# A Strassen MLP's first block: sums interleaved with x differences, w2's first casts moved to GpSimd, last stores moved to SyncE's queue

## The chip, the cores and the metric

The kernel runs on one core of one Trainium2 chip. The metric is the device time of one execution in microseconds (us), and smaller is better. "Median of n runs" is over the executions that were timed.

## The reference

```python
def reference(x, w1, w2):            # x [8, 1024, 1024], w1 [1024, 4096], w2 [4096, 1024], float32
    h = x @ w1
    h = 0.5 * h * (1 + np.tanh(np.sqrt(2 / np.pi) * (h + 0.044715 * h ** 3)))
    return (h @ w2).astype(np.float32)
```

## The kernel before

x is worked on in 8 superblocks of 1024 rows. Both matrix products use Strassen's scheme: 7 products of half-size blocks in place of 8, paid for with sums of weight blocks and differences of x blocks. Operands are 16-bit. (The second product of the first superblock is the exception, done with 8 plain products, as w2's sums are not made yet.)

The *first superblock* is unlike the others, and this case is about it. Besides its own products it loads w1 and w2 as float32, casts them, keeps w1's casts in DRAM (`raw_d`), makes w2's sums and stores them (`w_d`), casts the next superblock's x to 16 bits in DRAM (`x_cast`) and loads that transposed (`x_transpose`). The second superblock loads `raw_d` again and makes and stores w1's sums. From the third on, all sums come ready from DRAM.

Loads and most stores are issued by SyncE, in program order (`load_in_order`). GpSimd issues `x_cast`, the stores of w1's sums and the output's stores. Parts that the change touches (cuts marked `# ...`):

```python
up  = tile_pool(name="up", bufs=26)   # 16-bit units of 128x2048: x blocks, weights, sums ("u")
gcp = tile_pool(name="gcp", bufs=4)   # float32 staging tiles ("gc")
tp  = tile_pool(name="tp", bufs=10)   # 128x512 float32 results ("tmp")
# ...
def cast_in(dst, src, cast):          # float32 load into one of the 4 staging tiles, then a cast
    st = gcp.tile([P] + list(dst.shape[1:]), F32, name="gc")
    load_in_order(st, src)
    cast(out=dst, in_=st)
# ...
def load_cols(self, c, n):            # first quarter of w1, by columns
    cs = slice(c * P, (c + n) * P)
    for b, t in self.raw.items():
        # ... cast_in, blocks of the left half on ScalarE, of the right half on GpSimd
    for m in SUMS:
        self.sum(m, cs)
# ...
def x_first():
    # ... for each 128 rows:
            xn = gcp.tile([P, 2, HT], F32, name="gc")
            load_in_order(flat(xn), x2[r0:r0 + P, :])
            # ... transposed on TensorE, cast out of PSUM by ScalarE and DVE
# ...
def matmul2_first(sb, g, keep_w1, xb):
    for b in range(2):                                   # column halves of the output
        for q in range(NI // QC):                        # quarters of w2's rows
            # ... cast_in(raw..., w2v[...], nc.scalar.copy): w2 on ScalarE
            # ... products of this quarter into 8 banks
            if b == 0:
                # ... keep; if q == 0: keep_w1()
            else:
                # ... w2's sums on DVE
                if q in (1, 2):
                    write(q - 1)                         # 7 stores of 512 KB: w_d
        if b == 1:
            blocks = x_transpose(xb, load_in_order)      # 16 transposing loads
            write(2); write(3)
        for i in range(2 * NQ):
            # ... last 3 products of each bank, then
            o = temp()
            # ... copied out by ScalarE (i odd) or DVE (i even), and stored
# ...
blocks = x_first()
for sb in range(NSB):
    xs = x_sums(blocks)                                  # 5 differences on DVE
    g, quad = matmul1(xs, sb)
    if sb == 0:
        xb = x_cast(1, pool_last[0])                     # behind GpSimd's last cast so far
        last, blocks = matmul2_first(sb, g, quad.keep_raw, xb)
        continue
    # ...
```

Of the kernel before, what the change touches and what calls it, by code (L numbers as in the profile page):

```python
# [8 lines left out]
F32 = mybir.dt.float32  # L9
# [4 lines left out]
SUB = mybir.AluOpType.subtract  # L14
P = 128
# [38 lines left out]
def kernel(  # L54
# [48 lines left out]
    def unit(rows, cols):  # L103
        return up.tile([P, rows, cols], DT, name="u")

    def tt(out, in0, in1, op):
        nc.vector.tensor_tensor(out=out, in0=in0, in1=in1, op=op)  # L107
# [6 lines left out]
    def load_in_order(out, in_, **kw):  # L114
        return tc.keep_in_program_order(nc.sync.dma_start(out=out, in_=in_, **kw))  # L115
# [18 lines left out]
    def cast_in(dst, src, cast):  # L134
# [3 lines that stand above are left out]
# [4 lines left out]
    class MadeQuad:  # L142
# [22 lines left out]
        def load_cols(self, c, n):  # L165

            cs = slice(c * P, (c + n) * P)
            for b, t in self.raw.items():
                k0 = (int(b[0]) - 1) * KH
                for k in range(0, KH, KH // n):  # L170
                    cast_in(
                        t[:, k:k + KH // n, cs],
                        w1v[int(b[1]) - 1, :, k0 + k:k0 + k + KH // n, cs],
                        nc.scalar.copy if b[1] == "1" else pool_copy,
                    )
            for m in SUMS:
                self.sum(m, cs)

        def sum(self, m, sl=slice(None)):
            make_sum(self.ops, m, self.raw, KH, QW, sl)  # L180
# [18 lines left out]



    def x_sums(blocks):
        ops = {3: blocks["11"], 4: blocks["22"]}
        for m in (5, 1, 2, 7, 6):
            u, v = A_TERMS[m]
            ops[m] = unit(KH, HT)
            tt(ops[m], blocks[u], blocks[v], SUB)
        return ops

    def x_blocks():  # L210
        return {b: unit(KH, HT) for b in ("22", "21", "12", "11")}

    def x_first():
        identity = consts.tile([P, P], F32, name="identity")
        make_identity(nc, identity)
        blocks = x_blocks()
        for a in (1, 0):
            for q in range(NQ):
                r0 = a * HT + q * P
                xn = gcp.tile([P, 2, HT], F32, name="gc")  # L220
                load_in_order(flat(xn), x2[r0:r0 + P, :])
                for k in (1, 0):
                    ps = psum()
                    for j in range(KH):
                        nc.tensor.matmul(  # L225
                            ps[:, j * P:(j + 1) * P],
                            lhsT=xn[:, k, j * P:(j + 1) * P],
                            rhs=identity,
                            is_transpose=True,
                            start=(j == 0),  # L230
                            stop=(j == KH - 1),
                        )
                    eng = nc.vector.tensor_copy if k == 0 else nc.scalar.copy
                    eng(
                        out=blocks[f"{a + 1}{k + 1}"][:, :, q * P:(q + 1) * P],
                        in_=ps.rearrange("p (j t) -> p j t", t=P),
                    )
        return blocks

    def x_cast(s, after):  # L240
        xb = xdram.tile([SB, H], DT, name="xb")
# [19 lines left out]
    def matmul1(xs, sb):  # L261
        g = {b: gp.tile([P, NI, HT], GT, name=f"g{b}") for b in ("11", "12", "21", "22")}

        def product(bank, w, m, first, last):
            ops, cs = w
            for k in range(KH):
                nc.tensor.matmul(  # L267
                    bank,
                    lhsT=ops[m][:, k, cs],
                    rhs=xs[m][:, k, :],  # L270
                    start=(first and k == 0),
                    stop=(k == KH - 1),
                    skip_group_check=not first,
                )

        def gelu(b, c, src):
            nc.scalar.activation(out=g[b][:, c, :], in_=src, func=GELU)

        late = None

        def finish(c, w, q, s2):
            product(q, w, 6, False, True)
            c22 = temp()
            tt(c22, q, s2, ADD)
            gelu("22", c, c22)

        quads = []

        def ahead(q, step):

            if q == NI // QC:
                return
            if sb > 1:
                if step == 0:
                    quads.append(load_ops(w1_d[q], (4, 5, 1, 2, 3, 7, 6), KH, QW))
                return
            if step == 0:
                quad = MadeQuad(q, sb == 0)
                quads.append(quad)
                if sb == 0:  # L300
                    quad.load()
                    quads[q - 1].keep_raw()
            for m in ((), (4,), (1, 3), (7, 6))[step]:
                quads[q].sum(m)
            if sb == 1 and step == 3:
                quads[q].copy_plain()

        if sb == 0:
            quads.append(MadeQuad(0, True))
            for c, n in ((0, 1), (1, 1), (2, 2)):  # L310
                quads[0].load_cols(c, n)
        else:
            for step in range(QC):
                ahead(0, step)

        for c in range(NI):
            q, j = divmod(c, QC)
            if j == 0:
                ahead(q + 1, 0)
            w = (quads[q] if sb > 1 else quads[q].ops, slice(j * P, (j + 1) * P))  # L320
            pb, qb = psum(), psum()
            product(pb, w, 4, True, False)
            v = temp()
            nc.scalar.copy(out=v, in_=pb)  # L324
            product(qb, w, 5, True, False)
            u = temp()
            tt(u, v, qb, SUB)
            if late is not None:
                finish(*late)
            rb = psum()  # L330
            product(rb, w, 1, True, False)
            s = temp()
            tt(s, u, rb, ADD)
            product(pb, w, 2, False, True)
            gelu("21", c, pb)
            s2 = temp()
            tt(s2, s, pb, SUB)
            product(qb, w, 3, False, False)
            gelu("12", c, qb)
            product(rb, w, 7, False, True)  # L340
            c11 = temp()
            tt(c11, u, rb, ADD)
            gelu("11", c, c11)
            late = (c, w, qb, s2)
            if j:
                ahead(q + 1, j)
        finish(*late)
        return g, quads[-1]
# [3 lines left out]
    def store(sb, b, q, src):  # L352
        r0 = sb * SB + (int(b[0]) - 1) * HT + q * P
        o0 = (int(b[1]) - 1) * OH
        return nc.gpsimd.dma_start(out=out2[r0:r0 + P, o0:o0 + OH], in_=src)  # L355

    def matmul2_first(sb, g, keep_w1, xb):


        TAIL = 3  # L360
# [8 lines left out]
        for b in range(2):  # L369
# [13 lines left out]
            for q in range(NI // QC):  # L383
                raw = raw_units(QC, OH, (b + 1,))
                for j in range(0, QC, 2):
                    c = q * QC + j
                    for a in range(2):
                        cast_in(
                            raw[f"{a + 1}{b + 1}"][:, j:j + 2, :],
                            w2v[b, a, :, c:c + 2, :],  # L390
                            nc.scalar.copy,
                        )
                for j in range(QC):
                    w = [raw[f"{a + 1}{b + 1}"][:, j, :] for a in range(2)]
                    ready.append(w)
                    if q * QC + j < NI - TAIL:
                        for i in range(2 * NQ):
                            mm(i, q * QC + j, w)
                if b == 0:
                    keep.append(raw)  # L400
                    if q == 0:
                        keep_w1()
                else:
                    ops = {}
                    for m in SUMS + PLAIN:
                        make_sum(ops, m, {**keep[q], **raw}, QC, OH)
                    made.append(ops)
                    if q in (1, 2):
                        write(q - 1)
# [66 lines left out]
            last = store(sb, "11", q, c11)  # L476
        return last

    blocks = x_first()
    for sb in range(NSB):  # L480
        xs = x_sums(blocks)
        g, quad = matmul1(xs, sb)
        if sb == 0:
            xb = x_cast(1, pool_last[0])
            last, blocks = matmul2_first(sb, g, quad.keep_raw, xb)
            continue
        if sb + 1 < NSB:
            blocks = x_transpose(x_cast(sb + 1, last), nc.sync.dma_start)
        last = matmul2(sb, g)


# [28 lines left out]
```

## Time and profile before

| | before |
|---|---|
| time, median of 3 runs | 1620.16 us (1619.28 to 1620.61) |
| span of the profiled run | 1615.9 us |
| TensorE busy | 98% |
| first product starts | 26.73 us |
| time lost between the first and the last product, beyond 0.2157 us each | 19.2 us |
| from the start of the last product to the end of the span | 10.2 us |

TensorE (PE) issues 7296 matmuls: 64 transposes of x, then 7232 products of 512 columns, 0.2157 us apart when nothing holds them. That is 1560 us, and only the rest can be won.

PE's waits in the kernel before; the columns are what waited, the line, what it waited for, the total in us, how often, and the longest:

```profile
PE ps L267 <- ACT tmp L324: 8.9, 1, 8.9
PE ps L267 <- DVE u L107: 8.2, 1, 8.2
```

The wait of 8.2 us on DVE's `u` is the one before the first product. The one of 8.9 us on ScalarE's (ACT's) `tmp` is at 109.7 us. ACT's timeline shows what is behind it, GpSimd's (POOL's) and SyncE's what went on beside it (start, duration, engine, line, operation, count, and in brackets the idle time before and what ended it):

```profile
106.19 1.04 ACT L137 CAST u<-gc 128x1024 f16<-128x1024 f32 x1 [9.04 <-DMA gc<-in_w_dram]
```

```profile
88.00 4.06 POOL L244 DMA_DIRECT2D xb<-in_x_dram  x8
```

```profile
170.22 27.36 SPq L115 DMA_TRANSPOSE u<-xb  x16
...
214.33 1.08 SPq L152 DMA_DIRECT2D u<-raw_d_81  x1
```

ACT stood 9.04 us in front of a cast of w2 whose load (`gc<-in_w_dram`) had not landed, and since ACT takes its work in order, the copies behind it, for which PE waited, stood too. In that time the DMA engines carried GpSimd's x cast, issued at 88.00, in packets of 16 KB and 1.23 us each.

The last instructions of the kernel before:

```profile
1606.12 0.69 DVE L107 TENSOR_TENSOR tmp<-tmp,ps 128x512 f32<-128x512 f32 x1 [2.77 <-PE ps L439]
1607.10 0.54 POOL L355 DMA_DIRECT2D out_dram<-tmp  x1 [2.92 <-DVE tmp L107]
```

The last store is issued by GpSimd, whose closing drain then runs 8.06 us, to the end of the span at 1615.9.

### The profile page before, as it was taken

The numbers are of one execution on the slowest core, as the hardware profiler recorded it, in microseconds if no ns is written. First come the engines' busy times: TensorE is split into PE (matmuls) and PEld (weight loads), VectorE is DVE, ScalarE is ACT, GpSimd is POOL, SyncE is SP. The second block draws the span as 40 slices with busy tenths as digits, with TensorE's granted clock in tenths as the row PEclk, the third lists the DMA queues.
The fourth block names the chain that finished last, engine by engine and source line by source line (L and its number), as shares of the span: only waits on it lengthen the run. The fifth ranks groups of instructions, "written<-read, shape, count | busy, mean of one in ns | idle before, by whom it ended". The sixth has DMA issues, their size and how long they took to land.

```text
span 1615.9 us, 19003 instructions
## 1 busy us (share of the span) xinstructions
PE 1577.7 (98%) x7296; PEld 718.5 (44%) x7296; DVE 819.7 (51%) x1046; ACT 480.5 (30%) x794; POOL 135.0 (8%) x238
## 2 busy tenths in 40 slices
PE   6979999999999999999999999999999999999997
PEld 3434444444444444444444444444444444444443
DVE  5855345644455444555445554455434544455433
ACT  3656203431044210442114410244103431044210
POOL 2210112000110011000120001100011001000011
PEclk8999999999999999999999999999999999999999
DMA  6999999674566546546575555746557564535511
GB/s 224 350 311 329 297 389 320 181 292 150 206 207 182 235 170 217 164 153 261 179 225 144 175 232 192 241 118 242 197 209 217 135 269 148 198 137 183 208 53 53
DMA packets 160923, 338.91 MB, mean 210 GB/s; under 512 B 72384, under 2 KB 78528, under 8 KB 159936
## 3 DMA queue, kind: packets, MB, share of 16 engines
q1 hardware_dynamic: 144768, 274.77, 49.2%
q0 software_dynamic: 16064, 62.93, 12.0%
q8 instruction: 57, 0.93, 0.2%
q14 instruction: 34, 0.28, 0.1%
HBM read 266.34 MB, written 85.98 MB: 218 GB/s over the span
## 4 chain that ended last, share of the span: by engine, by line
PE 66%; issue 23%; DMA 5%; DVE 1%; POOL 1%; SPq 1%; ACT 1%; POOLq 0%; DVEq 0%; ACTq 0%
PE ps L267 33%; PE ps L439 30%; PE ps L375 3%; DMA gc<-in_w_dram 2%; DVE u L107 1%; POOL out_dram L355 1%; DMA u<-raw_d_82 1%; SPq L115 1%; DMA u<-raw_d_83 1%; DMA gc<-in_x_dram 1%; ACT u L137 1%; PE ps L225 0%; DMA xb<-in_x_dram 0%; DMA out_dram<-tmp 0%; SPq L152 0%
## 5 line engine op out<-in xcount | busy, mean ns | idle before, releaser
L267 PE MATMUL ps<-u 128*128 128x512 f16 x3584 | 780.3, 380 | 21.0 <-ACT tmp L324 8.9
L107 DVE TENSOR_TENSOR tmp<-tmp,ps 128x512 f32<-128x512 f32 x652 | 447.0, 687 | 667.9 <-PE ps L439 335.0
L267 PEld LDWEIGHTS <-u 128*128 128x128 f16 x3584 | 351.3, 98 | 448.8 <-issue 21.4
L439 PE MATMUL ps<-u,gc 128*128 128x512 f16 x2240 | 485.8, 379 | 0.0
L439 PEld LDWEIGHTS <-gc 128*128 128x128 bf16 x2240 | 219.3, 98 | 264.2
L355 POOL DMA_DIRECT2D out_dram<-tmp x128 | 69.3, 541 | 1313.9 <-ACT tmp L459 870.6
L107 DVE TENSOR_TENSOR u<-u 128x2048 f16<-128x2048 f16 (+2 forms) x110 | 123.2, 1151 | 58.1 <-ACT u L137 24.7
L324 ACT COPY tmp<-ps 128x512 f32<-128x512 f32 x128 | 72.9, 569 | 261.9 <-PE ps L267 261.8
L107 DVE TENSOR_TENSOR tmp<-ps,tmp 128x512 f32<-128x512 f32 x128 | 88.4, 690 | 5.9 <-PE ps L267 1.2
L459 ACT COPY tmp<-ps 128x512 f32<-128x512 f32 x28 | 16.4, 587 | 177.3 <-PE ps L439 177.3
L137 ACT CAST u<-gc 128x1024 f16<-128x1024 f32 (+1 forms) x52 | 50.2, 978 | 46.0 <-DMA gc<-in_w_dram 45.9
L375 PE MATMUL ps<-u,g_220 128*128 128x512 f16 x128 | 48.5, 379 | 0.0
L375 PE MATMUL ps<-u,g_221 128*128 128x512 f16 x128 | 48.5, 379 | 0.0
L375 PE MATMUL ps<-u,g_222 128*128 128x512 f16 x128 | 48.5, 379 | 0.0
L375 PE MATMUL ps<-u,g_223 128*128 128x512 f16 x128 | 48.5, 379 | 0.0
L465 ACT COPY tmp<-ps 128x512 f32<-128x512 f32 x28 | 16.4, 586 | 80.3 <-PE ps L439 80.3
L453 ACT COPY tmp<-ps 128x512 f32<-128x512 f32 x28 | 16.4, 586 | 74.9 <-PE ps L439 74.9
L244 POOL DMA_DIRECT2D xb<-in_x_dram x56 | 27.6, 514 | 14.4 <-DMA out_dram<-tmp 10.4
L118 POOL CAST u<-gc 128x1024 f16<-128x1024 f32 (+1 forms) x20 | 22.6, 1131 | 64.1 <-DMA gc<-in_w_dram 54.5
L419 ACT COPY tmp<-ps 128x512 f32<-128x512 f32 x8 | 4.7, 585 | 64.7 <-PE ps L375 64.7
L375 PEld LDWEIGHTS <-g_221 128*128 128x128 bf16 x128 | 12.5, 98 | 15.1
L375 PEld LDWEIGHTS <-g_223 128*128 128x128 bf16 x128 | 12.5, 98 | 15.1
(118 smaller groups left out, 846.5 us busy)
## 6 DMA issues: line engine op xcount, KB each, us to landing
out_dram<-tmp POOLq DMA_DIRECT2D x128, 256.0 KB, 3.6
gc<-in_w_dram SPq DMA_DIRECT2D x56, 512.0 KB, 6.1
u<-w_d_85 SPq DMA_DIRECT2D x49, 512.0 KB, 6.3
u<-w_d_86 SPq DMA_DIRECT2D x49, 512.0 KB, 6.9
u<-w_d_87 SPq DMA_DIRECT2D x49, 512.0 KB, 5.6
u<-w_d_88 SPq DMA_DIRECT2D x49, 512.0 KB, 6.1
u<-w_d_77 SPq DMA_DIRECT2D x42, 512.0 KB, 4.9
u<-w_d_78 SPq DMA_DIRECT2D x42, 512.0 KB, 5.2
```

What stands on the lines that cost most here:

```text
L107: nc.vector.tensor_tensor(out=out, in0=in0, in1=in1, op=op)
L118: pool_last[0] = nc.gpsimd.tensor_copy(out=out, in_=in_)
L137: cast(out=dst, in_=st)
L244: nc.gpsimd.dma_start(out=xb[q:q + P, :], in_=x2[s * SB + q:s * SB + q + P, :])
L267: nc.tensor.matmul(bank, lhsT=ops[m][:, k, cs], rhs=xs[m][:, k, :], start=(first and k == 0), stop=(k == KH - 1), skip_group_check=not first,)
L324: nc.scalar.copy(out=v, in_=pb)
L355: return nc.gpsimd.dma_start(out=out2[r0:r0 + P, o0:o0 + OH], in_=src)
L375: nc.tensor.matmul(banks[i], lhsT=g[f"{i // NQ + 1}{a + 1}"][:, c, (i % NQ) * P:(i % NQ + 1) * P], rhs=w[a], start=(c == 0 and a == 0), st ...
L439: nc.tensor.matmul(banks[q], lhsT=a[:, c, :], rhs=pieces[c // QC][:, c % QC, :], start=(first and c == 0), stop=(c == NI - 1), skip_group_ ...
L453: nc.scalar.copy(out=v[q], in_=ps)
L459: nc.scalar.copy(out=c21, in_=ps)
L465: nc.scalar.copy(out=c12, in_=ps)
```

## The change

The intent: bring the first product forward, keep ScalarE free of the stall near 100 us, and shorten the end.

1. **Front**: x is staged in tiles of the pool `up` and no longer in the four of `gcp`, so its loads don't wait for each other. The first w1 columns are loaded in fewer, larger pieces, and w1 sums and x differences alternate on DVE in the order in which products need them. Gelu's table is loaded at the start.
2. **w2**: the first 8 of w2's casts go from ScalarE to GpSimd, and the x cast is issued behind them.
3. **Stores**: the last superblock's stores go from GpSimd's queue to SyncE's.

The core of the diff (cuts marked `...`):

```diff
         def load_cols(self, c, n):
             cs = slice(c * P, (c + n) * P)
-            for b, t in self.raw.items():
-                k0 = (int(b[0]) - 1) * KH
-                for k in range(0, KH, KH // n):
-                    cast_in(...)
-            for m in SUMS:
-                self.sum(m, cs)
+            kn = 2 * KH // n
+            for b in range(2):
+                cast = (nc.scalar.copy, pool_copy)[b]
+                for k in range(2 * KH - kn, -1, -kn):
+                    st = gcp.tile([P, kn, n * P], F32, name="gc")
+                    load_in_order(st, w1v[b, :, k:k + kn, cs])
+                    for a in range(k // KH, (k + kn) // KH):
+                        cast(...)
+            return cs
...
-                xn = gcp.tile([P, 2, HT], F32, name="gc")
+                xn = up.tile([P, 2, HT], F32, name="u")
...
         if sb == 0:
             quads.append(MadeQuad(0, True))
-            for c, n in ((0, 1), (1, 1), (2, 2)):
-                quads[0].load_cols(c, n)
+            xs.make(5)
+            cs = quads[0].load_cols(0, 1)
+            quads[0].sum(4, cs)
+            for m in (1, 3, 7, 6):
+                if m != 3:
+                    xs.make(m)
+                quads[0].sum(m, cs)
+            for c, n in ((1, 1), (2, 2)):
+                cs = quads[0].load_cols(c, n)
+                for m in SUMS:
+                    quads[0].sum(m, cs)
...
-        return nc.gpsimd.dma_start(out=out2[r0:r0 + P, o0:o0 + OH], in_=src)
+        queue = nc.gpsimd if sb < NSB - 1 else nc.sync
+        return queue.dma_start(out=out2[r0:r0 + P, o0:o0 + OH], in_=src)
...
                             w2v[b, a, :, c:c + 2, :],
-                            nc.scalar.copy,
+                            pool_copy if b == 0 and q < 2 else nc.scalar.copy,
...
                     if q == 0:
                         keep_w1()
+                    elif q == 1:
+                        xb = x_cast(1, pool_last[0])
...
-    blocks = x_first()
+    warm = consts.tile([P, 1], F32, name="warm")
+    nc.vector.memset(warm, 0.0)
+    nc.scalar.activation(out=warm, in_=warm, func=GELU)
+    xs = x_first()
     for sb in range(NSB):
-        xs = x_sums(blocks)
         g, quad = matmul1(xs, sb)
         if sb == 0:
-            xb = x_cast(1, pool_last[0])
-            last, blocks = matmul2_first(sb, g, quad.keep_raw, xb)
-            continue
+            last, blocks = matmul2_first(sb, g, quad.keep_raw)
...
         if sb + 1 < NSB:
-            blocks = x_transpose(...)
-        last = matmul2(sb, g)
+            xs = XOps(blocks)
+            xs.make(5, 1, 2, 7, 6)
```

More of the change, by code (lines that the diff above doesn't have):

```diff
@@ L167, in load_cols @@
             cs = slice(c * P, (c + n) * P)
-            for b, t in self.raw.items():
-                k0 = (int(b[0]) - 1) * KH
-                for k in range(0, KH, KH // n):
-                    cast_in(
-                        t[:, k:k + KH // n, cs],
-                        w1v[int(b[1]) - 1, :, k0 + k:k0 + k + KH // n, cs],
-                        nc.scalar.copy if b[1] == "1" else pool_copy,
-                    )
-            for m in SUMS:
-                self.sum(m, cs)
+            kn = 2 * KH // n
[5 more added lines that the diff above has]
+                    for a in range(k // KH, (k + kn) // KH):
+                        cast(
+                            out=self.raw[f"{a + 1}{b + 1}"][:, :, cs],
+                            in_=st[:, a * KH - k:(a + 1) * KH - k, :],
+                        )
+            return cs
         def sum(self, m, sl=slice(None)):
@@ L198, in load_ops, with __init__, make @@
         return ops
-    def x_sums(blocks):
-        ops = {3: blocks["11"], 4: blocks["22"]}
-        for m in (5, 1, 2, 7, 6):
-            u, v = A_TERMS[m]
-            ops[m] = unit(KH, HT)
-            tt(ops[m], blocks[u], blocks[v], SUB)
-        return ops
+    class XOps(dict):
+        def __init__(self, blocks):
+            self.blocks = blocks
+            self[3], self[4] = blocks["11"], blocks["22"]
+        def make(self, *ms):
+            for m in ms:
+                u, v = A_TERMS[m]
+                self[m] = unit(KH, HT)
+                tt(self[m], self.blocks[u], self.blocks[v], SUB)
     def x_blocks():
@@ L237, in x_first @@
                     )
-        return blocks
+            if a:
+                xs.make(2)
+        return xs
     def x_cast(s, after):
@@ L354, in store, with matmul2_first @@
         o0 = (int(b[1]) - 1) * OH
-        return nc.gpsimd.dma_start(out=out2[r0:r0 + P, o0:o0 + OH], in_=src)
-    def matmul2_first(sb, g, keep_w1, xb):
+        queue = nc.gpsimd if sb < NSB - 1 else nc.sync
+        return queue.dma_start(out=out2[r0:r0 + P, o0:o0 + OH], in_=src)
+    def matmul2_first(sb, g, keep_w1):
         TAIL = 3
@@ L477, in matmul2 @@
         return last
-    blocks = x_first()
+    warm = consts.tile([P, 1], F32, name="warm")
+    nc.vector.memset(warm, 0.0)
+    nc.scalar.activation(out=warm, in_=warm, func=GELU)
+    xs = x_first()
     for sb in range(NSB):
-        xs = x_sums(blocks)
         g, quad = matmul1(xs, sb)
         if sb == 0:
-            xb = x_cast(1, pool_last[0])
-            last, blocks = matmul2_first(sb, g, quad.keep_raw, xb)
-            continue
+            last, blocks = matmul2_first(sb, g, quad.keep_raw)
+        else:
+            if sb + 1 < NSB:
+                blocks = x_transpose(x_cast(sb + 1, last), nc.sync.dma_start)
+            last = matmul2(sb, g)
         if sb + 1 < NSB:
-            blocks = x_transpose(x_cast(sb + 1, last), nc.sync.dma_start)
-        last = matmul2(sb, g)
+            xs = XOps(blocks)
+            xs.make(5, 1, 2, 7, 6)
 _INS = ['x', 'w1', 'w2']
```

## The prediction

> **What bounds it.** TensorE: 98% busy (page, part 1). Its 7232 matmuls of 512 columns start 0.2157 us apart at full clock, about 1560 of the 1615.9 us span. Only the rest can be won. The timeline of PE shows where it lies:
>
> - the first product starts at 26.73 us. The last x cast ends at 19.2; then DVE makes five x differences (1.22 us each) before the first w1 sum, whose end releases PE (wait of 8.2 us on DVE);
> - waits of 1.34 and 0.49 us at 41.7 and 53.7 us, then 8.9 us to 109.7 (on ACT's copy). There ACT stands 9.0 us before a cast of w2 that waits for its load, while the x cast's 16 KB packets (1.23 us each) fill the DMA engines from 92 to 104 us and 2 KB loads trickle. The Trainium skill, "DMA: Bandwidth & Descriptors", section on queues, rings and completion order, has each engine alternate between queues by packets; the trace agrees (about 20 such loads per us against about 190 alone);
> - half clock after both long gaps: matmuls 0.427 us apart, about 2.1 and 1.7 us lost;
> - the end: the last DVE sum ends at 1606.8, its store has landed by 1609.5, but GpSimd's closing drain runs 8.06 us from 1607.1 and holds the end back to 1615.9.
>
> From first product to the second matrix product (139.5 us) PE takes 113 us for 448 matmuls that need 96.7: 16.5 us lost.
>
> **What changes, costed.**
>
> 1. x loads no longer wait for four buffers: eight 512 KB loads at about 90 packets of 4 KB per us land by 14.3 us instead of 16.5; last x cast at 15.8. DVE then needs one difference (to 17.0) and the first sum (0.37): first product at 17.6 us, 9 earlier. The other differences stand between the sums. New waits: product 5 on GpSimd's w1 casts (1.3 to 1.7 us each beside DVE), 0.5 to 1 us; a temporary on DVE behind column 1's sums, about 1 us. Fewer, larger w1 loads run ahead of PE, so the waits at 41.7 and 53.7 go: 1.8 us.
> 2. Eight w2 casts go to GpSimd, the x cast behind them: I expect it on the DMA engines at 96 to 107 us. ACT's first w2 cast then needs a load issued before that; its fifth meets the x cast. Of 8.9 + 1.7 us I keep 1: about 9.6 gained.
> 3. Gelu's table loaded at the start: 1.3 us of ACT, off PE's path.
> 4. Last stores on SyncE's queue, behind loads all issued: GpSimd's drain runs early. The end comes 4 us after the last DVE sum instead of 9: 5 gained.
>
> Sum: 9 + 1.8 + 9.6 - 1.5 + 5, about 24 us, all on PE's path or the tail; the middle is unchanged.
>
> **Prediction: 1596.0 us (-1.5%)**, 8 in 10 between 1589 and 1603. Chances: faster by over 2% 0.06, within 2% 0.93, slower 0.01.
>
> **What would show it.** First product at 17 to 19 us; wait on ACT's copy near 90 to 110 us under 2 us; second product starting at 119 to 121 us; last DVE sum to end about 4 us; no PE gap after 125 us, as before.
>
> **What would make it wrong.** GpSimd's casts run later than thought, so the x cast collides with ACT's casts again (up to 9 us back); GpSimd's drain is a fixed cost at the end (5 back); slower w1 casts or loads in 512-byte pieces hold the first product (2 to 4 back); or the clock stays full through the start (2 more gained).

## More of the kernel before

SyncE's line is worth remembering for later: it has one list of transfers, and it starts the 16 transposing loads of x at 170.22 and the first `raw_d` load for the second superblock at 214.33.

The load on the DMA engines, from the windows view (length; PE busy and products; granted clock; DMA share, the mean busy share of the 16 engines; GB/s):

```profile
0.00:20.00 20.00, 11.14 (x64) 0.93 0.74 251
20.00:40.00 20.00, 13.27 (x52) 0.73 0.64 193
40.00:60.00 20.00, 18.00 (x81) 1.00 0.99 352
...
240.00:260.00 20.00, 18.41 (x87) 1.00 1.02 410
```

The engines are idle for a third of the first 40 us, and nearly full from 40 to 260 us (0.87 to 1.11 in every 20 us). Beyond 300 us the share is about 0.6.

## The result, and the profile after

The changed kernel takes **1605.38 us** (median of 4 runs, 1605.22 to 1609.44), the kernel before beside it 1619.81 (4 runs). The ratio is 0.9917, 95% interval 0.9899 to 0.9934. (Each ratio in this document is the mean time of one kernel's runs over that of the other's of the same rounds, so not quite the ratio of the medians quoted.) It is 14.4 us faster where 24 were predicted, and outside the range.

The two traces set side by side, product by product: I sort all matmuls by start time, number them (0 to 63 are the transposes, 64 is the first product, 512 the first of the second matrix product, 1024 the first of the second superblock) and subtract. "Predicted" is what the text says of the same stretch.

| stretch | before | after | difference | predicted |
|---|---|---|---|---|
| start of product 64 | 26.73 | 18.28 | -8.45 | -9 |
| 64 to 512 | 112.77 | 112.06 | -0.7 | -9.9 |
| 512 to 800 | 62.16 | 67.04 | +4.9 | 0 |
| 800 to 1072 | 60.74 | 58.71 | -2.0 | 0 |
| 1072 to the last product | 1343.30 | 1343.30 | 0 | 0 |
| last product to the end of the span | 10.23 | 4.36 | -5.9 | -5 |
| whole span | 1615.9 | 1603.7 | -12.2 | -24 |

The front and the end came as predicted. The 9.9 us between them did not, and a new loss of 4.9 us follows. The waits of PE after:

```profile
PE ps L277 <- ACT g_216 L287: 7.7, 2, 7.4
PE ps L233 <- DMA u<-in_x_dram: 4.6, 2, 4.3
PE ps L395 <- DVE tmp L443: 3.3, 1, 3.3
PE ps L277 <- DVE u L107: 2.9, 2, 2.5
```

The 8.2 us on DVE's `u` are now 2.9. The wait on ACT is still there, at 7.4 (now under the name `g_216`), and 3.3 us on a copy by DVE (L443) are new. ACT, POOL and SyncE answer to the lines shown of before:

```profile
118.76 1.04 ACT L137 CAST u<-gc 128x1024 f16<-128x1024 f32 x1 [8.00 <-DMA gc<-in_w_dram]
```

```profile
98.54 1.04 POOL L118 CAST u<-gc 128x1024 f16<-128x1024 f32 x1 [6.13 <-DMA gc<-in_w_dram]
...
103.52 4.06 POOL L254 DMA_DIRECT2D xb<-in_x_dram  x8
```

```profile
160.05 26.67 SPq L115 DMA_TRANSPOSE u<-xb  x16
...
202.99 4.79 SPq L152 DMA_DIRECT2D u<-raw_d_81  x4
```

GpSimd's second four casts of w2 had to wait 6.13 us for their load, which stood behind the copies of w1 on SyncE's queue. So the x cast was issued at 103.52 and was on the DMA engines from 106.9 us, eleven later than I had thought, and met ACT's next casts instead of the first ones: 8.00 us of idle time before the cast at 118.76. The same stall, 12.6 us later. SyncE is 10 us ahead of before at the transposes (160.05 against 170.22) and 11 at the first `raw_d` load.

```profile
181.91 0.69 DVE L443 COPY tmp<-ps 128x512 f32<-128x512 f32 x1 [1.90 <-PE ps L395]
189.80 1.23 DVE L107 TENSOR_TENSOR u<-u 128x2048 f16<-128x2048 f16 x1 [7.20 <-DMA u<-xb]
190.95 0.68 DVE L443 COPY tmp<-ps 128x512 f32<-128x512 f32 x1
```

The lines that answer to them in the kernel before:

```profile
193.66 0.69 DVE L421 COPY tmp<-ps 128x512 f32<-128x512 f32 x1 [1.90 <-PE ps L375]
200.37 5.89 DVE L107 TENSOR_TENSOR u<-u 128x2048 f16<-128x2048 f16 x5 [6.02 <-DMA u<-xb]
```

This is the new wait. DVE stands at the first of the second superblock's x differences (L107), which waits 7.20 us for the transposed x to land, and the copy out of a PSUM bank (PSUM holds TensorE's results; L443, 190.95), for which PE waits, is behind it in DVE's order. In the kernel before the four copies (the last at 193.66) came first and the five differences after them. The change creates the differences at another place in the program, and the scheduler put one ahead of the last copy.

```profile
0.00:20.00 20.00, 11.67 (x68) 1.00 0.96 313
20.00:40.00 20.00, 17.93 (x72) 0.91 0.93 299
```

The DMA engines are now full from the start: 0.96 and 0.93 in the first 40 us where it was 0.74 and 0.64. And the end:

```profile
1599.81 0.69 DVE L107 TENSOR_TENSOR tmp<-tmp,ps 128x512 f32<-128x512 f32 x1 [2.77 <-PE ps L461]
1600.53 0.33 SPq L375 DMA_DIRECT2D out_dram<-tmp  x1
```

The last store goes out by SyncE at 1600.53, GpSimd's closing drain (8.88 us here) ran at 1407, and the span ends 3.2 us after DVE's last sum.

### The profile page after: what moved, and what is told of

Same layout as the page of the kernel before. It is cut to its first block, busy times and chain, and to the rows that moved or that the text cites. A ratio compares the mean times of both kernels' runs of the same rounds, so it can differ in the third digit from the quotient of the medians.

```text
span 1603.7 us, 18985 instructions
## 1 busy us (share of the span) xinstructions
PE 1578.2 (98%) x7296; PEld 717.9 (45%) x7296; DVE 819.6 (51%) x1047; ACT 472.3 (29%) x784; POOL 132.1 (8%) x228
## 4 chain that ended last, share of the span: by engine, by line
PE 95%; DMA 3%; DVE 1%; ACT 1%; issue 0%; SPq 0%; POOL 0%; DVEq 0%
PE ps L277 46%; PE ps L461 42%; PE ps L395 7%; DMA gc<-in_w_dram 2%; DVE u L107 1%; ACT u L137 0%; DVE tmp L107 0%; DMA u<-in_x_dram 0%; DMA u<-xb 0%; SPq L115 0%; POOL u L118 0%; ACT g_218 L287 0%; ACT g_216 L287 0%; ACT g_217 L287 0%; ACT tmp L343 0%
## 5 line engine op out<-in xcount | busy, mean ns | idle before, releaser
L107 DVE TENSOR_TENSOR tmp<-tmp,ps 128x512 f32<-128x512 f32 x652 | 447.1, 687 | 661.6 <-PE ps L461 333.3
L375 POOL DMA_DIRECT2D out_dram<-tmp x112 | 60.6, 542 | 1108.0 <-ACT tmp L481 733.9
L107 DVE TENSOR_TENSOR u<-u 128x2048 f16<-128x2048 f16 (+2 forms) x110 | 123.0, 1152 | 56.6 <-ACT u L137 21.5
L107 DVE TENSOR_TENSOR tmp<-ps,tmp 128x512 f32<-128x512 f32 x128 | 88.4, 691 | 5.9 <-PE ps L277 1.2
L137 ACT CAST u<-gc 128x1024 f16<-128x1024 f32 x36 | 37.2, 1044 | 37.6 <-DMA gc<-in_w_dram 37.6
L118 POOL CAST u<-gc 128x1024 f16<-128x1024 f32 (+1 forms) x26 | 28.5, 1105 | 73.8 <-DMA gc<-in_w_dram 60.0
L395 PEld LDWEIGHTS <-g_218 128*128 128x128 bf16 x128 | 12.6, 98 | 18.8 <-issue 3.9
L395 PEld LDWEIGHTS <-g_215 128*128 128x128 bf16 x128 | 12.6, 99 | 15.5 <-issue 0.8
## 6 DMA issues: line engine op xcount, KB each, us to landing
out_dram<-tmp POOLq DMA_DIRECT2D x112, 256.0 KB, 4.4
```

The lines of the kernel that those rows point to most:

```text
L107: nc.vector.tensor_tensor(out=out, in0=in0, in1=in1, op=op)
L118: pool_last[0] = nc.gpsimd.tensor_copy(out=out, in_=in_)
L375: return queue.dma_start(out=out2[r0:r0 + P, o0:o0 + OH], in_=src)
L395: nc.tensor.matmul(banks[i], lhsT=g[f"{i // NQ + 1}{a + 1}"][:, c, (i % NQ) * P:(i % NQ + 1) * P], rhs=w[a], start=(c == 0 and a == 0), st ...
```

## The experiments

I started from three theories for the missing 10 us:

- **The x cast.** The stall of ACT follows the x cast: whatever load ACT's casts need while the 16 KB packets pass comes late. Moving it moves the stall.
- **The order.** The wait at 188 us comes of the x difference ahead of the copy, and would go with it.
- Formed after the first eight runs, as the first two did not pay: **the bytes.** The transfers of the first 255 us as a whole set the pace, and a wait taken away comes back further down.

The runs came each with the kernel before in the same rounds. They fell on different chips, where the kernel before has medians from 1619.6 to 1622.8, so the ratios to it are the yardstick. One trace of a kernel scatters too: in two traces of the same kernel (`early_cast` and `early_again`) product 1072 starts 3.5 us apart.

For `half_cast`, `extra_early`, `extra_late` and `early_order_actq` there are two traces. The figures and lines below are of the first, whose spans (1601.7, 1608.5, 1606.5 and 1610.7 us) belong to the profiled runs. The trace kept with each run is of another execution that is not among the times listed (spans 1598.8, 1608.6, 1601.9 and 1609.1 us); where it is used, it is called the kept trace. Product 1072 of `extra_late` starts at 258.9 us in the first and at 254.3 in the kept one, 4.6 us apart.

### The three parts alone: front_only, w2_only, stores_only

`front_only` undoes parts 2 and 3, `w2_only` is before with part 2, `stores_only` is before with part 3, by the hunks shown above.

> The start of the change alone: x in free units, differences and w1 sums interleaved, w1 loads merged, Gelu's table first. w2's casts are all on ACT again, the x cast is behind the last w1 cast, stores are on GpSimd's queue. Theory (the w2 part of the change moved ACT's stall behind an x cast, it did not take it away): first product at 18.3 us as in the whole change, ACT's stall back near 90 us with PE waiting 8 to 10 us, nothing near 115; time 1610 to 1613. Rival (the w2 part gained its 9 us and another thing, such as w2 loads late behind the raw copies, took them later): the stall near 115 us is there too, time 1618 or more.

> GpSimd's eight w2 casts with the x cast behind them, alone in the kernel before. Theory: the wait near 100 us goes and one of 6 to 10 us comes some 15 us later, where ACT casts the third quarter of w2 while the x cast fills the DMA engines: 1616 to 1622, no clear gain. Rival (the stall near 115 us comes from the start running ahead of the loads): here the start is the old one, so no stall: 1609 to 1611.

> The last stores on SyncE's queue, alone in the kernel before. From the two traces: end of the last DVE sum to the end of the span falls from 9.1 to 3.2 us, so 5.9 us: 1613.5 to 1614.5. If GpSimd's closing drain only moved work, less than 3 us.

| run | time (before beside it: 1621.77) | ratio, 95% interval |
|---|---|---|
| front_only | 1614.17 | 0.9955, 0.994 to 0.997 |
| w2_only | 1619.10 | 0.9989, 0.9976 to 1.0002 |
| stores_only | 1614.07 | 0.9963, 0.9944 to 0.9982 |

The gain of the change is the front (some 7 us) and the stores (some 6). **Part 2 gives nothing that these runs can tell from zero.** In the trace of `w2_only`, the stall before product 400 is gone (it starts 8.75 us earlier than before's), and then PE waits:

```profile
99.69 25.84 PE L267 MATMUL ps<-u 128*128 128x512 f16 x117
134.10 1.44 PE L267 MATMUL ps<-u 128*128 128x512 f16 x3 [8.56 <-ACT g L277]
```

PE ran from 99.69 for 117 products and then waited 8.56 us for ACT. At product 496 the run is 2 us behind the kernel before. `front_only` shows the other half: the wait on ACT is at its old place (7.0 us near 99 us), and the wait on DVE's copy near 190 us is there (4.1 us). So this wait came with part 1, in which the differences moved, and not with part 2.

### The order mended: order_fix

```diff
-            xs = XOps(blocks)
-            xs.make(5, 1, 2, 7, 6)
+            xs = XOps(blocks)
+            with tc.issue_after(evicted[0].ins):     # the first half's last copy by DVE
+                xs.make(5, 1, 2, 7, 6)
```

(The hunk is moved to the first superblock's branch; `evicted[0]` is set where DVE copies.)

> The whole change, with the second block's x differences issued on DVE only after the last copy out of the first half's banks. Theory: the wait of 3.3 us at 188 us and the half clock after it (1.3 us) come from that order alone, as the copy stood behind a difference that waited for the transposes: both go, 1600 to 1601.5. Rival (PE there waits for w2's second half, or for the copy itself): the wait stays, 1604 to 1606.

1606.96 us, ratio 0.9914 (0.9900 to 0.9928): no gain on the changed kernel's 0.9917. The wait at 188 us is gone from the trace as intended, but:

```profile
251.29 2.97 PE L277 MATMUL ps<-u 128*128 128x512 f16 x13 [2.62 <-DVE tmp L107]
```

```profile
250.55 1.47 DVE L107 TENSOR_TENSOR tmp<-tmp,ps 128x512 f32<-128x512 f32 x2 [3.69 <-DMA out_dram<-tmp]
```

PE now waits 2.62 us at 251 us, for DVE, which waits for a `tmp` tile whose store to the output (`out_dram<-tmp`) has not landed. In the trace of the changed kernel there is no wait there. The theory of the order described the wait rightly and predicted the time wrongly.

### The x cast elsewhere, or in smaller packets: late_cast, late_and_order, early_cast, small_packets

```diff
 # late_cast
-                            pool_copy if b == 0 and q < 2 else nc.scalar.copy,
+                            pool_copy if b == 0 and (q < 2 or (q, j, a) == (3, 2, 1)) else nc.scalar.copy,
-                    elif q == 1:
+                    elif q == 3:
                         xb = x_cast(1, pool_last[0])
 # late_and_order: the same, with order_fix
 # early_cast: x_cast back before matmul2_first, w2's casts stay on GpSimd
 # small_packets: each transfer of the first x cast in two half rows
-                nc.gpsimd.dma_start(out=xb[q:q + P, :], in_=x2[s * SB + q:s * SB + q + P, :])
+                for h in range(0, H, HT):
+                    nc.gpsimd.dma_start(out=xb[q:q + P, h:h + HT], in_=x2[..., h:h + HT])
```

> The changed kernel with the x cast behind one more GpSimd cast, the last of w2's first half, so that it is issued near 120 us and not at 103.5, when ScalarE has no cast left whose load could be held up. Theory (the x cast's transfer holds up a load that ScalarE's casts need, wherever it falls among them): the 7.4 us wait for ScalarE's g near 123 us goes, the wait for DVE's bank copy near 188 us (3.3) grows by 0 to 5 us because x lands later; time 1596 to 1602. Rival (the loads are late because GpSimd's casts free their buffers late, x cast or not): a wait of 5 us or more for ScalarE stays near 115 to 125 us, time 1604 or more.

> The same, and the second block's x differences put behind the first half's last bank copies. Theory: neither the wait for ScalarE near 123 us nor that for DVE's copy near 188; some 3 us of wait for a store's tile near 250 us as in the run with the order alone; time 1593 to 1600. Rival (the reordering gives nothing because the later wait takes it all): no better than the late cast alone, within 2 us.

> The changed kernel with the x cast where it was before the change (ahead of w2's casts on GpSimd), w2's casts still on GpSimd. Theory (a stall follows the x cast, wherever it is among w2's loads): the wait moves back from 123 us to 90 to 105 us and keeps 6 to 9 us, time 1602 to 1608. Rival (moving w2's casts to GpSimd would have been enough, it was the place of the x cast that spoiled it): the wait is under 3 us, time 1597 to 1600.

> The changed kernel with the first x cast written in half rows: twice the transfers on GpSimd's queue, and packets that can't take in several rows, so 16 KB packets of 1226 ns become packets of 2 KB or less. Theory (the loads starve because a packet of the x cast takes an engine eight times as long as one of theirs, and the two queues take turns by packet): the loads keep a third to a half of their rate, the ScalarE stall of 8.0 us shrinks to 1 to 4, the PE wait of 7.4 us to 0 to 3; time 1597 to 1602. Rival (it is the bytes, or the issue order on one queue, that hold the load up): stall 7 us or more, time 1604 or more.

| run | time (before: 1622.83) | ratio, 95% interval | longest wait of PE on ACT | on DVE, 180 to 255 us |
|---|---|---|---|---|
| late_cast | 1608.65 | 0.9914, 0.9896 to 0.9932 | 1.6 | 11.1 at 194 |
| late_and_order | 1607.79 | 0.9912, 0.9895 to 0.9929 | 1.0 | 4.35 at 242, 5.90 at 250 |
| early_cast | 1604.67 | 0.9891, 0.9873 to 0.9909 | 4.9 | 3.0 at 191 |
| small_packets | 1607.14 | 0.9907, 0.9886 to 0.9927 | 3.2 | 2.9 at 190 |

This is where the first two theories failed *as explanations of the time*. `late_cast` did what it was made for: the stall is 1.6 us, not 7.4, product 512 starts 5.4 us earlier than in the changed kernel. All of it is lost 70 us later:

```profile
194.03 54.20 PE L395 MATMUL ps<-u,g 128*128 128x512 f16 x244 [11.10 <-DVE tmp L443]
```

The x transposes, issued by SyncE from 164 us on (159.7 to 164.4 in the traces of the table below with these transfers), have not landed when PE comes to the last copies, and now it stands 11.1 us before them. With the order mended too (`late_and_order`) PE is 11.8 us ahead of the changed kernel at product 800, and loses it all again 50 us further:

```profile
241.86 1.86 PE L277 MATMUL ps<-u 128*128 128x512 f16 x4 [4.35 <-DVE tmp L107]
249.62 10.65 PE L277 MATMUL ps<-u 128*128 128x512 f16 x36 [5.90 <-DVE tmp L107]
```

```profile
240.38 0.53 POOL L192 DMA_DIRECT2D w_d<-u  x1 [8.91 <-DMA u<-raw_d]
...
243.39 3.33 POOL L375 DMA_DIRECT2D out_dram<-tmp  x6
```

GpSimd's queue has stood 8.91 us for a `raw_d` load to land. The output stores stand behind it, and the tiles they free are what DVE waits for, and PE for DVE.

`small_packets` tests the mechanism of the stall itself. The x cast's packets were 16,384 bytes and 1.23 us, now they are 1,024 bytes; ACT's idle time in front of one cast fell from 8.00 to 2.93 us. That fits what the Trainium skill says and my prediction leant on ("DMA: Bandwidth & Descriptors", Queues, rings and completion order): each engine goes round between its queue rows by whole packets. That long packets of one row leave less to the other is my inference from it, and the traces agree: beside the x cast, w2's loads moved about 33 packets of 2 KB per us in the changed kernel (107 to 119 us) and about 87 with the small packets. But the x cast itself then took 22.6 us and not 12.9, the loads behind came late in turn (PE waited 1.45, 3.18 and 1.27 us), and the time is unchanged.

### Bytes added and taken away: half_cast, extra_early, extra_late

```diff
 # half_cast (wrong result on purpose)
-            for q in range(0, SB, P):
+            for q in range(0, SB // 2 if s == 1 else SB, P):      # and both transposes read these rows
 # extra_early: in matmul2_first, second half, behind the second quarter
+                    if q == 1:
+                        extra = xdram.tile([4, P, QC * OH], DT, name="extra")
+                        for i in range(4):
+                            nc.gpsimd.dma_start(out=extra[i], in_=flat(made[0][SUMS[i]]))
 # extra_late: in the second superblock's second product, behind each of 4 stores
+            if sb == 1:
+                nc.gpsimd.dma_start(out=extra[q, 0], in_=c21)
+                nc.gpsimd.dma_start(out=extra[q, 1], in_=c21)
```

> Wrong result on purpose: the changed kernel with only the first half of x's second superblock cast, and both halves of the transposes reading it. That takes 4 of 8 transfers, some 5 us of all 16 DMA engines, out of the first 200 us and changes no order. New theory (the DMA engines, busy 0.93 to 1.03 of every 20 us from the start to 260 us, and not any one wait, bound the first 200 to 250 us; a wait taken away comes back behind): SyncE starts the x transposes near 155 and not 160 us, the waits of PE shrink by 3 to 6 us in all, time 1599 to 1602. Rival (each wait has its own cause, such as ScalarE's order, and this half of the x cast in the same place holds up the same load): the wait for ScalarE's g shrinks by under 2 us and the one at 188 us stays, time 1603 or more.

> The changed kernel with four needless 512 KB stores, some 5.4 us of all DMA engines at the rate the trace shows for such packets, put on GpSimd's queue, which is idle there, between 130 and 160 us; nothing waits for them. New theory: SyncE's x transposes start about 5 us later than 160, the wait for DVE's copy near 188 us grows from 3.3 to 6 to 9 us, time 1608 to 1612. Rival: these stores are on no chain, no wait grows by more than 1 us, time 1604 to 1606.5.

> The control: the same 2.1 MB of needless stores on GpSimd's queue near 375 to 390 us, where the DMA engines are busy about 0.55 of the time. Both theories: nothing waits, time within 1.5 us of the changed kernel, 1604 to 1607. If it costs 3 us or more, extra bytes cost time for another reason than that the engines are full.

| run | time (before: 1621.24) | ratio, 95% interval |
|---|---|---|
| half_cast (wrong result) | 1603.20 | 0.9890, 0.9876 to 0.9903 |
| extra_early | 1612.65 | 0.9945, 0.9932 to 0.9959 |
| extra_late | 1606.82 | 0.9913, 0.9899 to 0.9926 |

`extra_early` is the clearest run. Four stores that nothing waits for, on a queue that had nothing else to do, cost 5.8 us against the control with the same bytes near 380 us, and the intervals do not touch. The trace shows the way: SyncE, which has nothing to do with these stores, starts the transposes at 165.66 us, later than in any trace of the same transfers without them (160.1 to 164.4), and the wait at 189 us is 6.5 us where the changed kernel has 3.3 and 3.0, the control 2.0:

```profile
165.66 26.59 SPq L115 DMA_TRANSPOSE u<-xb  x16
```

```profile
PE ps L277 <- ACT g L287: 8.3, 2, 7.9
PE ps L395 <- DVE tmp L447: 6.5, 1, 6.5
```

The same two lines of the control, `extra_late`:

```profile
163.97 25.47 SPq L115 DMA_TRANSPOSE u<-xb  x16
```

```profile
PE ps L395 <- DVE tmp L443: 2.0, 1, 2.0
```

The kept traces agree (transposes from 165.08 us and a wait of 7.5 us, against 161.12 and 2.4) and show how the stores reach SyncE. SyncE has eight transfers in flight at most: each issue waits for the landing of the one eight places before it. In `extra_early` the first transpose was issued 0.07 us after such a landing, of a store of w2's sums, and the 14 of those stores ahead of it took 11.1 us on the mean from issue to landing, where the control's took 9.1. The needless stores themselves had landed by 149.5 us, so it was not that they held tiles which the transposes needed.

What the two share is the DMA engines (and the memory behind them). One limit of this test: the loss came by way of the wait that `order_fix` takes away (product 800 starts 5.0 us later than in the changed kernel, and from there to product 1072 both take 58.7 us). What the same stores cost with the order mended was not run.

`half_cast` takes away a similar amount of the engines' time, earlier: 3.6 us faster than the control in time, but SyncE starts the transposes at 159.2, hardly earlier and not at 155 as I expected, and both waits stay (4.8 and 3.4). In its kept trace SyncE starts them at 157.3, the waits are 1.5 and 3.0, and product 1072 starts at 250.8. I count it for the bytes in direction, not in size.

### A first try at a better version: early_order_actq

```diff
 # early_cast and order_fix, and in store():
+        if sb == 0 and b[1] == "2":
+            queue = nc.scalar
```

> A try at a better version: the x cast at its old place, the second block's x differences behind the last bank copies, and the first block's second half of stores on ScalarE's queue and not behind w1 sums' stores on GpSimd's. New theory: the transfers stay the same, so the gain is small: a wait that goes comes back within some 60 us, time 1601 to 1606. Rival (the waits at 188 and 248 us were each of an order that this mends): no PE wait over 1.5 us behind 140 us, time 1594 to 1600.

1611.73 us, ratio 0.9942: worse, and by a mistake of mine. The next x cast is held back only by an order behind the `last` store *on the same engine*. With that store on ScalarE, the order held nothing, and the second x cast was issued right behind the first, from 88 us on. It is a doubled x cast by accident, and as such it fits the mechanism of the stall:

```profile
123.93 1.04 ACT L137 CAST u<-gc 128x1024 f16<-128x1024 f32 x1 [17.11 <-DMA gc<-in_w_dram]
```

17.11 us of idle time, where `early_cast` with one x cast has 6.64. No wait over 1.1 us came after it, and product 1072 was at 263.0. It says nothing of the question that it was made for.

### Bytes taken away later, orders mended, and the changed kernel again: less_early, order_actq, tr_before_actq, after_again

```diff
 # less_early (wrong result on purpose): w2's second half, last two quarters
+                    if b == 1 and q >= 2:
+                        # ... one load serves both casts: 4 loads of 512 KB fall away
 # order_actq: changed kernel with order_fix, and 7 of the 8 stores of that half
+        if sb == 0 and b[1] == "2" and (b, q) != ("22", NQ - 1):
+            queue = nc.scalar
 # tr_before_actq: order_actq, and x_transpose ahead of write(1)
-                    if q in (1, 2):
-                        write(q - 1)
+                    if q == 1:
+                        write(0)
                 blocks = x_transpose(xb, load_in_order)
+                write(1)
                 write(2)
```

> Wrong result on purpose: the changed kernel in which w2's last two quarters of the second half are loaded once for both halves of their rows, so 4 loads of 512 KB fall away between 135 and 160 us, some 5.4 us of all DMA engines; casts and everything else stay. DMA theory: SyncE starts the x transposes near 154 to 156 and not 160 us, the wait of 3.3 us at 188 us goes, 2.5 to 5 us faster than the changed kernel beside it (1600 to 1603). Rival (the order of the x difference ahead of the bank copy holds it whatever the bytes): the wait stays at 2 us or more, under 1 us faster.

> The changed kernel with the second block's x differences behind the first half's last bank copies, and 7 of the 8 stores of the second half of the first block on ScalarE's queue, so that they don't wait on GpSimd's queue behind stores of w1 sums. DMA theory: bytes are the same, the loss comes back within 80 us as a wait for loads or tiles of 1.5 us or more, within 2 us of the changed kernel. Rival (each wait was an order's): no wait over 1 us behind 140 us, 3.5 to 5.5 us faster than the changed kernel.

> The same, and SyncE's x transposes ahead of the second set of w2 sums' stores, so that x lands some 7 us earlier. DMA theory: as above, within 2 us of the run before it. Rival: as good as the run before it or up to 1 us better, with the DVE copies at 175 to 190 us waiting for nothing but PE.

> The changed kernel itself, unchanged, as the base for the three others on this chip: 1604.5 to 1608, waits as in its first profile.

| run | time (before: 1619.55) | ratio, 95% interval |
|---|---|---|
| less_early (wrong result) | 1603.41 | 0.9900, 0.9886 to 0.9915 |
| order_actq | 1605.23 | 0.9909, 0.9894 to 0.9924 |
| tr_before_actq | 1647.52 | 1.0167, 1.0153 to 1.0181 |
| after_again | 1606.92 | 0.9921, 0.9907 to 0.9934 |

`less_early` is 3.5 us faster than the changed kernel beside it, as the bytes would have it, and the wait at 190 us shrank from 3.0 to two of 0.7. But the two intervals overlap, its profiled run was its slowest (1606.45) with a stall of 10.0 us, and in that trace product 1072 is not earlier and SyncE starts the transposes at 160.2 us, not at 154 to 156 as I expected. It supports the theory without proving it.

`order_actq` has neither of the two orders any more, and PE's wait is back all the same:

```profile
256.21 4.05 PE L277 MATMUL ps<-u 128*128 128x512 f16 x18 [2.31 <-DVE tmp L107]
```

The chain of waits shows what it ends on (start, duration, what):

```profile
243.01 12.34 DMA out_dram<-tmp
```

A store of 256 KB, issued by ScalarE as soon as its tile was written and behind no one's wait, needed 12.34 us to land. `order_actq` is 1.7 us faster than the changed kernel, inside the scatter. Here it is a transfer that is slow, not an order that is bad.

`tr_before_actq` failed: SyncE waits 44.3 us, until 202 us, for PE's products, which still read the units that the transposes load into, and PE then stands 42.2 us. Which units come free first hangs on the order in which they are handed out, and my edit changed it. As a test of the order it is void.

### The best of them again: early_again, early_actq2

`early_again` is `early_cast` unchanged; `early_actq2` is `order_actq` with the x cast at its old place.

> The x cast at its old place, as in the earlier run of the same kernel: ratio 0.988 to 0.991 of the kernel before, 1603 to 1606, if its lead of about 2 us was more than scatter; 0.991 to 0.993 if not.

> The early x cast, the second block's x differences behind the last bank copies and 7 stores on ScalarE's queue (the last of the 8 stays on GpSimd's queue, as its order holds back the next x cast). DMA theory: product 1072 past the start, near 252 to 256 us in every correct version so far, stays there, time within 1.5 us of the run beside it. Rival: 3 to 5 us faster than it, 1599 to 1602.

1607.15 us, ratio 0.9913 (0.9895 to 0.9930), and 1604.70, ratio 0.9898 (0.9881 to 0.9916), with 1621.45 for the kernel before. The lead of `early_cast` was scatter. `early_actq2`: its interval overlaps that of the changed kernel (0.9907 to 0.9934). **No version was shown to beat the changed kernel.**

### All traces in one table

Start times of four products, and of SyncE's first x transpose, in us, worked out from the traces as above (for `extra_late` and `extra_early` from the first ones):

| kernel | 64 | 512 | 800 | 1072 | x transposes |
|---|---|---|---|---|---|
| before | 26.7 | 139.5 | 201.7 | 262.4 | 170.2 |
| stores_only | 25.4 | 143.2 | 205.3 | 268.1 | 173.6 |
| w2_only | 26.6 | 141.0 | 203.2 | 263.5 | 172.5 |
| front_only | 18.0 | 132.9 | 201.0 | 259.7 | 162.9 |
| after | 18.3 | 130.3 | 197.4 | 256.1 | 160.1 |
| after_again | 17.8 | 130.5 | 197.2 | 255.9 | 161.3 |
| extra_late | 17.3 | 133.8 | 198.1 | 258.9 | 164.0 |
| order_fix | 18.0 | 133.7 | 195.8 | 257.3 | 163.2 |
| order_actq | 17.8 | 132.9 | 195.0 | 256.2 | 162.3 |
| small_packets | 17.7 | 129.4 | 196.3 | 255.3 | 159.7 |
| early_cast | 17.6 | 130.7 | 197.6 | 256.3 | 161.2 |
| early_again | 17.5 | 132.6 | 201.2 | 259.9 | 163.0 |
| early_actq2 | 17.9 | 133.0 | 195.1 | 256.0 | 163.3 |
| late_cast | 18.3 | 124.9 | 199.7 | 258.6 | 164.4 |
| late_and_order | 17.2 | 122.6 | 185.5 | 258.4 | 161.4 |
| extra_early | 17.8 | 131.4 | 202.4 | 261.1 | 165.7 |

Behind product 1072 all of them run to the end with 1.0 to 1.6 us lost. So column 1072 is the time, but for the tail. The twelve traces from `front_only` to `late_and_order`, all with the new front and the same transfers, are 11 us apart at product 512, 16 us apart at product 800, and within 4.6 us (255.3 to 259.9) at product 1072, which is no more than the two traces of `extra_late` differ. PE's lead was not kept in any of these orders.

## Why the prediction was right or wrong

**Right: "first product at 17.6 us, 9 earlier".** It came at 18.28, 8.45 earlier, and between 17.0 and 18.3 in all traces with the new front.

**Right: "4 us after the last DVE sum instead of 9: 5 gained".** It was 3.2 us after, 5.9 gained in the trace, and `stores_only` shows the part alone at 0.9963.

**About right: the small waits.** I set 1.5 us of new waits against 1.8 us of old ones. In the first 60 us after the first product, PE's start-to-start gaps of over 0.6 us and the half clock (a stretch in which the throttle grants TensorE half its clock) cost about 4.9 us, against about 4.25 before. These are estimates: each gap less 0.2157 us, plus half of what remained of the half-clock record. So about 0.65 us were lost and not 0.3 gained.

**Wrong: "Of 8.9 + 1.7 us I keep 1: about 9.6 gained".** This is the term of the sum that failed first. The wait was 7.4 us and the half clock followed it again. I had the x cast "at 96 to 107 us" on the DMA engines; it was issued at 103.52 and on the engines from 107 to 120. GpSimd's casts had to wait for loads behind w1's copies in SyncE's queue. I had named this risk ("the x cast collides with ACT's casts again (up to 9 us back)") and it happened, at nearly the full size. The part alone (`w2_only`) gave 0.9989, within its interval of nothing.

**Wrong: "no PE gap after 125 us, as before".** A wait of 3.3 us at 188 us is new, 4.9 us lost in that stretch with the half clock behind it. The listing of DVE's new order showed a `L107` between two copies, and I took it for one of w2's sums.

**The error beneath both.** I wrote "Only the rest can be won", looked for the rest in PE's waits, and added up those that the change removes, as if each wait were a cost by itself. The runs show otherwise. None of the versions built here got the 9.6 us: `late_cast` took the stall away and got 11.1 us of wait at 194 us for it, `late_and_order` took that away as well and got 10.25 us at 242 and 250 us. That the transfers set the pace is shown best by `extra_early`, within the limit named there: 2.1 MB on another queue at 131 to 150 us cost 5.8 us against the same at 380 us, which cost nothing that the runs can tell. From 120 to 260 us, with shares of 0.93 to 1.05 in every 20 us of the changed kernel's windows view, the DMA engines have little room; behind 300 us, with 0.6 on the mean, they do.

Seen so, the gain of the front is what it did for the DMA engines: idle for about 12 of the first 40 us before, for about 2 after (from the shares in the windows: 20 x (0.26 + 0.36) against 20 x (0.04 + 0.07)). All transfers behind came 10 us earlier (SyncE's column), and of this PE kept 6.3 at product 1072. That is a figure of two single traces: `stores_only`, which is the kernel before up to its last stores, has 268.1 there and the kernel before 262.4. Versions without the new front reach it at 262 to 268, those with it and the same transfers at 254 to 260. That the removed idle time is *the* reason is argued from this table, not shown by a run of its own.

**What stays open.** How much of the 10 us PE really keeps; what extra bytes cost once the order is mended; and the stretch before 130 us, where `half_cast` took away 5 us of transfers and SyncE came 1 us earlier in one trace and 3 in the other. There the four staging tiles and the orders of ACT and GpSimd can hold the loads back too (the DMA share in `late_cast` is 0.81 from 100 to 120 us), and no run separates them from the engines. Nor do the runs tell the DMA engines apart from the memory behind them.

**Half clock.** I counted it with the gaps, as the Trainium skill has it ("TensorE: Matmul & The Clock Gate", Part 1: about 3.4 us idle is enough, and 426.7 against 215.7 ns from start to start). The traces agree on the spacing (matmuls 0.427 and 0.2157 us apart), and the half-clock records last 3.41 us or multiples of it (6.83, 10.24, 13.65). On the gap they put the limit a little lower: idle time of 3.34 us (changed kernel, at 188 us) and of 3.02 us (`after_again`, `early_cast`) was followed by a record, 3.00 us (kept trace of `half_cast`) and 2.31 us (`order_actq`) by none. The length doesn't follow from the gap alone: 6.83 us with an idle time of 8.90 us (before), 10.24 us with one of 4.94 us (`early_cast`).

## What to carry to other kernels

A wait of the busiest engine is a gain only if what feeds it can feed it earlier: before adding waits up, look at the DMA share of every stretch up to the point where the engine last waits, and ask what the next thing needed will be and when it lands. Where the transfers are the limit, count bytes and idle time of the DMA engines, not the places where the compute engine stands. The cheap test for it is a needless transfer on an idle queue, once in the stretch in question and once where the engines have room: if only the first costs time, as here, expect little from reordering; none of the orders tried paid.

## What the Trainium skill lacked or had wrong

- "DMA: Bandwidth & Descriptors", on queues, rings and completion order, says that engines switch queues by packets, and elsewhere that a packet is preferably at most 4,096 bytes. What it lacks is the size that a casting DRAM-to-DRAM transfer of whole contiguous rows makes: here 16,384 bytes and 1.23 us each, which held ACT up for 8 to 10 us; in half rows they were 1,024 bytes and the stall in front of one cast fell from 8.00 to 2.93 us.
- No page that I know of gives what a needless transfer on one queue costs the others when all 16 engines are near full. Here 2.1 MB on GpSimd's queue cost 5.8 us by way of SyncE's transposes, and nothing that the runs can tell where the share was near 0.6.
- No page that I know of has the closing drain of GpSimd behind its software transfers: 8.06 us (before, at the end of the span) and 8.88 us (after, at 1407 us). It was in no one's way once another engine issued the last stores.
- "TensorE: Matmul & The Clock Gate" (Part 1) puts the idle time that leads to the half clock at about 3.4 us. Here 3.02 us were enough in two traces, and 3.00 us were not in a third.
